# A two-block model at 256 tokens: the buffers of the main matmuls begin 64 bytes apart modulo 512 in place of on one edge

## The chip, the cores and the metric

The kernel runs on one core of one Trainium2 chip. The metric is the device time of one execution in microseconds (us); the time before is the median of three runs, 2506.98 us (2501.33 to 2507.89).

## The reference

Two residual blocks run one after the other on 256 tokens of width 2048, in float32. Cut to what matters:

```python
# block 1: attention in a sliding window, then SwiGLU
x = x + sliding_window_attention(rms_norm(x), w_qkv, ...) @ w_o
x = x + (silu(h @ w_gate) * (h @ w_up)) @ w_down          # D_FF = 5632
# block 2, layer 0: mLSTM mixer
proj = modulate(rmsnorm(x)) @ a_w_in                      # 16400 columns
x = x + gate * rmsnorm(mlstm(proj) @ a_w_out)
# block 2, layer 1: attention over bands of chunks
kv = modulate(rmsnorm(x)) @ kv_w                          # 4096 columns
x = x + gate * rmsnorm(band_attention(h @ b_w_in, kv) @ b_w_out)
```

The modulations come from a vector c times ada_w_2 and kv_ada_w_2, which the kernel sums on VectorE. Nearly all arithmetic is in the eight large products, of a 256-row activation with a weight matrix read from HBM.

## The kernel before, in words

**Precision.** Each float32 operand of a large product is split into a high part of the type float32r and a float32r remainder, and a product is three matmuls: high by high, high by low, low by high. The activations' parts stand in four lasting buffers of 16 tiles of 128 x 256: `xh` and `xl` (the normed input) and `ah` and `al` (the mixers' and the FFN's inner result). They are the lines 117 to 120.

**The weights' stream.** A weight matrix goes through in pieces of 256 rows by 512 columns (512 KB). `stream_load` (line 138) has SyncE's queue fetch a piece into one of three buffers `w`; `stream_split` (line 146) has ScalarE cast it into `wh` and VectorE subtract it into `wl`, each with four buffers that are used in turn. `do_group` (line 226) loads up to four pieces and splits up to three pieces ahead of the one in use.

**The main matmuls.** `products` (line 267) issues them, in one of two modes. In the mode "tok" the activation part is stationary (128 x 128) and 512 columns of the weight part move past it; in "wst" 128 columns of the weight part are stationary and the 256 tokens move:

```python
PE.matmul(o, h[:, c], wh[:, k], ...)      # tok
PE.matmul(o, h[:, c], wl[:, k], ...)
PE.matmul(o, l[:, c], wh[:, k], ...)
PE.matmul(o, wh[:, k, cc], h, ...)        # wst
PE.matmul(o, wh[:, k, cc], l, ...)
PE.matmul(o, wl[:, k, cc], h, ...)
```

In the profile the moving operand is named first: `mm<-wh,xh` is tok, `mm<-xh,wh` is wst. Each matmul has a weight load of its own (PEld), which runs while the matmul before it streams; what TensorE reads at one time is thus the moving operand of one matmul and the stationary one of the next. TensorE starts main matmuls in the order written, with smaller ones between them (named `bg`: transposes, attention scores, gates).

**Where the buffers stand.** The tiles are laid out in order of allocation. `xh` begins at byte 34816 of each partition, which is 68 times 512; each of `xh`, `xl`, `ah`, `al` and `big` is 16384 bytes, and each buffer of `w`, `wh` and `wl` is 4096 bytes, so all of these begin at 0 modulo 512. The slices that one matmul reads (512 bytes of a stationary part, 1024 or 2048 of a moving one) begin at 0 modulo 512 as well. Of the operands of other float32r matmuls, `onesr` begins at 128, `acch` and `accl` at 448 modulo 512, and slice kt of `wgh` and of `wgl` at 416 + 160 kt.

**Order of the work.** It is worked out when the program is built: a model of the engines' clocks (`Clock`, `Eng`) decides at which main matmul a background task advances. The model looks at the number of elements and the type, not at addresses. A second stream of pieces (`mvt`) feeds the modulation sums on VectorE (`mvacc`).

**The end.** The last product, b_w_out, writes 512 columns of two token tiles at a time; `fin_half` (line 1235) squares them on ScalarE for a sum (`sumsq`, line 458), with the squares themselves written to a junk tile `sq` that nothing reads.

Of the kernel before, what the change touches and what calls it, by code (L numbers as in the profile page):

```python
# [10 lines left out]
F32 = mybir.dt.float32  # L11
F32R = mybir.dt.float32r
# [6 lines left out]
P = 128  # L19
D = 2048  # L20
T = 256
KD = D // P
SL = 2
CW = 512
NEG = -1.0e30
EPS = 1e-6
DFF = 5632
# [53 lines left out]
def kernel(ctx: ExitStack, tc: tile.TileContext, i: dict, out: bass.AP):  # L81
# [5 lines left out]
    keep = ctx.enter_context(tc.tile_pool(name="keep", bufs=1))  # L87
    strm = ctx.enter_context(tc.tile_pool(name="strm", bufs=1))
    rest = ctx.enter_context(tc.tile_pool(name="rest", bufs=1))
    small = ctx.enter_context(tc.tile_pool(name="small", bufs=4))  # L90
    psp = ctx.enter_context(tc.tile_pool(name="psp", bufs=8, space=PSUM))

    live = [0, 0]
    mmres = [4]
    ver = {"x": [0] * KD, "a": [0] * KD}
# [18 lines left out]
    onesr = keep.tile([P, P], F32R, name="onesr")  # L114
    mods = keep.tile([P, 3, 2, KD], F32, name="mods")
    x = keep.tile([P, 2, D], F32, name="x")
    xh = keep.tile([P, KD, T], F32R, name="xh")
    xl = keep.tile([P, KD, T], F32R, name="xl")
    ah = keep.tile([P, KD, T], F32R, name="ah")
    al = keep.tile([P, KD, T], F32R, name="al")  # L120
    big = keep.tile([P, 2 * D], F32, name="big")
    raw = big.rearrange("p (k t) -> p k t", t=T)
    part = big.rearrange("p (t n) -> p t n", t=2)
# [14 lines left out]
    def stream_load(upto):  # L138
        while cnt["load"] < min(upto, len(order)):
            ch, s = order[cnt["load"]]  # L140
            w = strm.tile([P, SL, CW], F32, tag="w", bufs=3, name="w")
            ch.load(s, w)
# [3 lines left out]
    def stream_split(upto):  # L146
        while cnt["split"] < min(upto, len(order)):
            j = cnt["split"]
            w = loaded.pop(j)
            clk.cur = 0.0  # L150
            wh = strm.tile([P, SL, CW], F32R, tag="wh", bufs=4, name="wh")
            S.copy(wh, w)
            wl = strm.tile([P, SL, CW], F32R, tag="wl", bufs=4, name="wl")
            V.tensor_sub(wl, w, wh.bitcast(F32))
            split[j] = (wh, wl, clk.cur)
            cnt["split"] += 1
# [54 lines left out]
    def wload(w, r0, c0):  # L211
        def f(s, t):
            a = w[r0 + s * SL * P:r0 + (s + 1) * SL * P, c0:c0 + CW]
            nc.sync.dma_start(out=t, in_=a.rearrange("(k p) n -> p k n", p=P))
# [11 lines left out]
    def do_group(idxs):  # L226
        staged = len(idxs) > 1
        ch, s0 = order[idxs[0]]
        for k in range(s0 * SL, (s0 + len(idxs)) * SL):
            while ver[ch.need[0]][k] < ch.need[1][k]:  # L230
                stall()
        stream_load(idxs[0] + 1 + PF)
        stream_split(idxs[0] + 1 + SP)
        if s0 == 0:
            shp = [P, CW] if ch.mode == "tok" else [P, 2, T]
            while live[0] + live[1] > 6:
# [3 lines left out]
        for ts in ((0,), (1,)) if staged else ((0, 1),):  # L240
            for j, idx in enumerate(idxs):
                s = order[idx][1]
                if j and ts[0]:
                    stream_load(idx + 1 + PF)
                    stream_split(idx + SP)
                wh, wl, t_w = split.pop(idx) if ts[-1] else split[idx]
                for k in range(SL):
                    kt = s * SL + k
                    clk.cur = max(t_w, rdy[ch.need[0]][kt])
                    products(ch, kt, k, wh, wl, ts)  # L250
                    ch.k = kt + ts[-1]
                    if not staged:
                        mv_step()
                    if kt < ch.nk - 1:
                        pump()
            if s == ch.ns - 1:
                clk.cur = clk.eng["pe"]
                if ch.part is not None:
                    for t in ts:
                        ch.part(ch.ps, t)  # L260
                if ts[-1]:
                    if not (ch.done and ch.done(ch.ps)):
                        mm_free()
                    ch.ps = None
                pump()
# [52 lines left out]
    def mv_jobs():  # L318
        for lab, w, c0, b, kind, dst in (
                [("A", i["ada0"], j * CW, i["ada_b"][0:1, j * CW:(j + 1) * CW], "col", (0, j // 4, j % 4))  # L320
                 for j in range(8)]
# [134 lines left out]
        return b.rearrange("p a b -> p (a b)")  # L456

    def sumsq(junk_pool, src, dst, scale=1.0):
        j = junk_pool.tile([P, CW], F32, tag="sq", bufs=1, name="sq")
        S.activation(j, src, ACTF.Square, scale=scale, accum_out=dst)  # L460

    def xt_pair(m):
# [83 lines left out]
    ssx = rest.tile([P, 2, 4], F32, name="ssx")  # L546
# [208 lines left out]
    def resid(n, ps, pool, after):  # L755
        for t in range(2):
            c = x[:, t, n * CW:(n + 1) * CW]
            V.tensor_add(c, ps[t], c)
            sumsq(pool, c, ssx[:, t, n:n + 1])
        add_bg(after(n))  # L760
# [36 lines left out]
    pools = {}  # L797
# [50 lines left out]
    def down_part(ps, t):  # L848
        c = x[:, t, 3 * CW:]
        V.tensor_add(c, ps[t], c)  # L850
        sumsq(pools["q2"], c, ssx[:, t, 3:4])
        if t:
            add_bg(xt_raw(3, raw))
# [146 lines left out]
    def num_task(h, v):  # L1000
# [22 lines left out]
        for t in range(2):  # L1023
            sumsq(q3, nm[t], ss[:, t:t + 1], scale=rd[:, t:t + 1])
# [143 lines left out]
    def band_head(g, j):  # L1168
# [5 lines left out]
        nc.sync.dma_start(out=bi, in_=bass.AP(tensor=rel.tensor, offset=h * 383, ap=[[1, P], [1, T]]))  # L1174
        G.memset(bi[0:64, 0:64], NEG)
        yield 1
# [57 lines left out]

    def fin_half(ps, t, n):
        c = pools["yy"][:, t, n * CW:(n + 1) * CW]
        sumsq(pools["q4"], ps[t], ssx[:, t, n:n + 1])
        V.tensor_mul(c, ps[t], gt[1][:, n * CW:(n + 1) * CW])

    def fin_done(n):  # L1240
        def f(ps):
            for t in range(2):
                fin_half(ps, t, n)
        return f

    def fin_part(ps, t):
        fin_half(ps, t, 3)
        x_rstd((t,))
        for n in range(4):
            c = x[:, t, n * CW:(n + 1) * CW]  # L1250
            y = pools["yy"][:, t, n * CW:(n + 1) * CW]
            if n == 3:
                S.activation(y, y, ACTF.Copy, scale=rst[:, t:t + 1])
                G.tensor_add(c, c, y)
            else:
                V.scalar_tensor_tensor(c, y, rst[:, t:t + 1], c, op0=ALU.mult, op1=ALU.add)
        for n in range(4):
            nc.sync.dma_start(out=out[t * P:(t + 1) * P, n * CW:(n + 1) * CW], in_=x[:, t, n * CW:(n + 1) * CW])
# [39 lines left out]
    S.activation(warm, ones[:, 0:1], ACTF.Exp)  # L1298
    stream_load(1)
    stream_split(1)  # L1300
    load_x(0)
    nc.sync.dma_start(out=cols, in_=i["cols"])
# [35 lines left out]
def _lay(inputs):  # L1338
# [10 lines left out]
    r = np.arange(P)  # L1349
    lo = np.where(r[None, :] <= r[:, None], f(0), f(NEG)).astype(f)  # L1350
    up = np.where(r[None, :] > r[:, None], f(0), f(NEG)).astype(f)
    ge = np.where(r[None, :] >= r[:, None], f(0), f(NEG)).astype(f)
    inv = np.power(10000.0, -np.arange(0, 64, 2) / 64.0).astype(f)
# [33 lines left out]
```

## Time and profile before

| | |
|---|---|
| median of three runs | 2506.98 us |
| the profiled execution | 2509.79 us |
| its span, first to last instruction | 2508.0 us |
| mean granted TensorE clock in it | 0.989 |
| TensorE busy | 2438.4 us (97%) |
| VectorE busy | 1752.8 us (70%) |
| ScalarE busy | 1210.1 us (48%) |
| DMA queue of the weights | 573.42 MB, 70.8% of 16 engines |

A matmul's shown duration is longer than its share of TensorE, since matmuls are pipelined: a row "0.39" may follow the one before it by 0.23 us. What one matmul costs is therefore read from start to start. The timeline gives starts to 0.01 us, so a distance is taken over many matmuls and divided by their number. [...]

### The profile page before, as it was taken

The page shows a single profiled execution, that of the slowest core. Times are in us where ns is not written, and L with a number is a line of the kernel's source. Part 1 is how long each engine was busy: PE and PEld are TensorE (multiplying, and loading weights), DVE is VectorE, ACT ScalarE, POOL GpSimd, SP SyncE. Part 2 cuts the span into 40 slices and gives each one's busy share as a digit, 9 for nine tenths or more (in the row PEclk, how much of TensorE's full clock was granted, in tenths as well). Part 3 has the DMA queues.
Part 4 walks back from the last instruction along what each step waited for, and adds up shares of the span by engine and source line. Part 5 has one row for each costly group of instructions (what it writes and reads, how often), then busy time and mean ns, then how long its engine had stood idle before and what let it go on. Part 6 is the DMA issues. An engine that isn't in the chain of part 4 may idle for free.

```text
span 2508.0 us, 34570 instructions
## 1 busy us (share of the span) xinstructions
PE 2438.4 (97%) x12782; PEld 2076.4 (83%) x12782; DVE 1752.8 (70%) x2577; ACT 1210.1 (48%) x1654; POOL 173.4 (7%) x174
## 2 busy tenths in 40 slices
PE   8989999999999999899999999999999899999998
PEld 6867888887888888778888788888888789899986
DVE  6885777777777777768778777755454664577765
ACT  5665544334443444554445444445444544555553
POOL 0232000000000000201101100101101120000000
PEclk9989999999999999999999999999999999999999
DMA  6524788888888887568878788856556456678854
GB/s 211 157 96 143 238 285 284 286 275 279 287 283 291 285 286 267 159 213 269 264 250 273 267 286 277 261 170 192 182 169 196 151 151 186 193 254 263 259 188 153
DMA packets 319226, 575.63 MB, mean 230 GB/s; under 512 B 21680, under 2 KB 56752, under 8 KB 319056
## 3 DMA queue, kind: packets, MB, share of 16 engines
q1 hardware_dynamic: 319056, 573.42, 70.8%
q8 instruction: 100, 1.64, 0.3%
q14 instruction: 70, 0.57, 0.1%
HBM read 571.25 MB, written 2.10 MB: 229 GB/s over the span
## 4 chain that ended last, share of the span: by engine, by line
PE 77%; DVE 7%; DMA 6%; issue 4%; ACT 4%; POOL 2%; SPq 0%; ACTq 0%; DVEq 0%; POOLq 0%
PE mm L66 72%; PE bg L66 5%; DVE wl L66 3%; ACT wh L66 2%; DMA w<-in_a_w_in_dram 2%; DVE mvacc L66 2%; DMA w<-in_w_gate_dram 1%; DMA w<-in_w_down_dram 1%; POOL big L66 1%; DMA w<-in_w_qkv_dram 1%; ACT big L66 1%; POOL y L66 0%; DMA w<-in_a_w_out_dram 0%; POOL so L66 0%; ACT sq L66 0%
## 5 line engine op out<-in xcount | busy, mean ns | idle before, releaser
L66 DVE TENSOR_TENSOR wl<-w,wh 128x1024 fp32r<-128x1024 f32 x816 | 1009.3, 1244 | 620.9 <-ACT wh L66 605.4
L66 ACT CAST wh<-w 128x1024 fp32r<-128x1024 f32 x816 | 854.9, 1051 | 957.1 <-PE mm L66 598.8
L66 PE MATMUL mm<-wh,xh 128*128 128x512 f32 x1760 | 691.4, 393 | 0.0
L66 PE MATMUL mm<-wh,xl 128*128 128x512 f32 x1760 | 686.8, 390 | 3.8 <-DVE xl L66 3.8
L66 PE MATMUL mm<-wl,xh 128*128 128x512 f32 x1760 | 686.8, 390 | 3.0 <-DVE wl L66 3.0
L66 DVE SCALAR_TENSOR_TENSOR mvacc<-mvt,sc,mvacc 128x512 f32<-128x512 f32 x512 | 392.2, 766 | 10.1 <-issue 0.5
L66 PEld LDWEIGHTS mm<-wh,xl 128*128 128x128 f32 x1760 | 331.1, 188 | 74.3 <-DVE xl L66 4.7
L66 PEld LDWEIGHTS mm<-wl,xh 128*128 128x128 f32 x1760 | 331.2, 188 | 72.2 <-DVE wl L66 5.1
L66 PEld LDWEIGHTS mm<-wh,xh 128*128 128x128 f32 x1760 | 331.2, 188 | 70.5 <-issue 2.6
L66 PE MATMUL mm<-xh,wh 128*128 128x256 f32 x1280 | 370.0, 289 | 7.9 <-DVE xh L66 7.9
L66 PE MATMUL mm<-xl,wh 128*128 128x256 f32 x1280 | 367.5, 287 | 1.0 <-DVE xl L66 0.9
L66 PE MATMUL mm<-xh,wl 128*128 128x256 f32 x1280 | 365.6, 286 | 0.0
L66 PE MATMUL mm<-wh,al 128*128 128x512 f32 x864 | 337.8, 391 | 3.5 <-DVE al L66 3.5
L66 PE MATMUL mm<-wh,ah 128*128 128x512 f32 x864 | 340.3, 394 | 0.0
L66 PE MATMUL mm<-wl,ah 128*128 128x512 f32 x864 | 337.5, 391 | 0.0
L66 PEld LDWEIGHTS mm<-xh,wh 128*128 128x128 f32 x1280 | 249.2, 195 | 11.6 <-DVE xh L66 5.5
L66 PEld LDWEIGHTS mm<-xl,wh 128*128 128x128 f32 x1280 | 249.1, 195 | 4.4 <-DVE xl L66 3.5
L66 PEld LDWEIGHTS mm<-xh,wl 128*128 128x128 f32 x1280 | 249.1, 195 | 0.0
L66 PEld LDWEIGHTS mm<-wh,al 128*128 128x128 f32 x864 | 163.0, 189 | 38.1 <-DVE al L66 3.9
L66 PEld LDWEIGHTS mm<-wh,ah 128*128 128x128 f32 x864 | 162.9, 189 | 36.7 <-issue 3.3
L66 PEld LDWEIGHTS mm<-wl,ah 128*128 128x128 f32 x864 | 163.0, 189 | 33.2 <-DVE wl L66 0.3
L66 POOL TENSOR_TENSOR so<-so,sz 128x512 f32<-128x512 f32 x16 | 29.6, 1851 | 711.8 <-DVE mvacc L66 361.8
(191 smaller groups left out, 1303.2 us busy)
## 6 DMA issues: line engine op xcount, KB each, us to landing
mvt<-in_ada_dram SPq DMA_DIRECT2D x192, 512.0 KB
w<-in_a_w_in_dram SPq DMA_DIRECT2D x192, 512.0 KB
w<-in_w_gate_dram SPq DMA_DIRECT2D x88, 512.0 KB
w<-in_w_up_dram SPq DMA_DIRECT2D x88, 512.0 KB
w<-in_w_down_dram SPq DMA_DIRECT2D x88, 512.0 KB
mvt<-in_kv_ada_dram SPq DMA_DIRECT2D x64, 512.0 KB
w<-in_a_w_in_dram SPq DMA_DIRECT2D x128, 256.0 KB
w<-in_a_w_out_dram SPq DMA_DIRECT2D x64, 512.0 KB
```

Source lines behind the costliest of these rows:

```text
L66: return fn(*a, **k)
```

## The change

A helper `stepped` allocates a tile with 16 more float32 elements (64 bytes) in a row than are used and hands out the front. The four activation parts and the four buffers each of `wh` and `wl` are made with it, so that each pushes what is allocated behind it 64 bytes further: modulo 512, `xh`, `xl`, `ah`, `al` begin at 0, 64, 128, 192; `big` and the three `w` at 256; the four `wh` at 256, 320, 384, 448; the four `wl` at 0, 64, 128, 192. What is allocated later moves by 768 bytes, which is 256 modulo 512. So that it all fits, the junk tile `sq` of the last stage (2048 bytes) is given up and `fin_half` writes the squares into the first two tiles of `xh`. Numbers of instructions, shapes, loops and DMAs are as before.

```diff
+STEP = 16
...
+    def stepped(pool, k, n, **kw):
+        t = pool.tile([P, k * n + STEP], F32R, **kw)
+        return t[:, 0:k * n].rearrange("p (k n) -> p k n", n=n)
...
-    xh = keep.tile([P, KD, T], F32R, name="xh")
-    xl = keep.tile([P, KD, T], F32R, name="xl")
-    ah = keep.tile([P, KD, T], F32R, name="ah")
-    al = keep.tile([P, KD, T], F32R, name="al")
+    xh, xl, ah, al = (stepped(keep, KD, T, name=n) for n in ("xh", "xl", "ah", "al"))
...
-            wh = strm.tile([P, SL, CW], F32R, tag="wh", bufs=4, name="wh")
+            wh = stepped(strm, SL, CW, tag="wh", bufs=4, name="wh")
             S.copy(wh, w)
-            wl = strm.tile([P, SL, CW], F32R, tag="wl", bufs=4, name="wl")
+            wl = stepped(strm, SL, CW, tag="wl", bufs=4, name="wl")
...
     def sumsq(junk_pool, src, dst, scale=1.0):
-        j = junk_pool.tile([P, CW], F32, tag="sq", bufs=1, name="sq")
+        if junk_pool is None:
+            j = xh[:, 0:2].rearrange("p k t -> p (k t)")
+        else:
+            j = junk_pool.tile([P, CW], F32, tag="sq", bufs=1, name="sq")
...
-        sumsq(pools["q4"], ps[t], ssx[:, t, n:n + 1])
+        sumsq(None, ps[t], ssx[:, t, n:n + 1])
```

## Rows read from the trace of the kernel before

**Rows 1.** The page's head and its busy times by engine.

```profile
span 2508.0 us, 34570 instructions
PE 2438.4 (97%) x12782; PEld 2076.4 (83%) x12782; DVE 1752.8 (70%) x2577; ACT 1210.1 (48%) x1654; POOL 173.4 (7%) x174
```

**Rows 2.** The page's chain that ended last, by line.

```profile
PE mm L66 72%; PE bg L66 5%; DVE wl L66 3%; ACT wh L66 2%; DMA w<-in_a_w_in_dram 2%; DVE mvacc L66 2%; DMA w<-in_w_gate_dram 1%; DMA w<-in_w_down_dram 1%; POOL big L66 1%; DMA w<-in_w_qkv_dram 1%; ACT big L66 1%; POOL y L66 0%; DMA w<-in_a_w_out_dram 0%; POOL so L66 0%; ACT sq L66 0%
```

**Rows 3.** The page's groups of main matmuls: moving operand, stationary operand, shape, number, then busy us and mean ns of one.

```profile
L66 PE MATMUL mm<-wh,xh 128*128 128x512 f32 x1760 | 691.4, 393 | 0.0
L66 PE MATMUL mm<-wh,xl 128*128 128x512 f32 x1760 | 686.8, 390 | 3.8 <-DVE xl L66 3.8
L66 PE MATMUL mm<-wl,xh 128*128 128x512 f32 x1760 | 686.8, 390 | 3.0 <-DVE wl L66 3.0
...
L66 PE MATMUL mm<-xh,wh 128*128 128x256 f32 x1280 | 370.0, 289 | 7.9 <-DVE xh L66 7.9
L66 PE MATMUL mm<-xl,wh 128*128 128x256 f32 x1280 | 367.5, 287 | 1.0 <-DVE xl L66 0.9
L66 PE MATMUL mm<-xh,wl 128*128 128x256 f32 x1280 | 365.6, 286 | 0.0
L66 PE MATMUL mm<-wh,al 128*128 128x512 f32 x864 | 337.8, 391 | 3.5 <-DVE al L66 3.5
L66 PE MATMUL mm<-wh,ah 128*128 128x512 f32 x864 | 340.3, 394 | 0.0
L66 PE MATMUL mm<-wl,ah 128*128 128x512 f32 x864 | 337.5, 391 | 0.0
```

**Rows 4.** An unbroken stretch of tok matmuls in the FFN: two of TensorE's rows of the timeline (start us, duration us, ...), the first and the last of 566, and the busy times of all engines between them (PE, PEld, DVE, ACT, POOL, each with its number of instructions; then granted clock, DMA share, GB/s). The 565 of the window are those from the first row to the last but one.

```profile
732.70 0.39 PE L66 MATMUL mm<-wl,ah 128*128 128x512 f32 x1
...
860.77 0.39 PE L66 MATMUL mm<-wh,xl 128*128 128x512 f32 x1
...
733.00:860.70 127.70, 127.70 (x565) 105.75 (x564) 97.36 (x107) 50.67 (x50) 1.58 (x3) 1.00 0.86 289
```

**Rows 5.** The same for an unbroken stretch of wst matmuls in the keys of the last layer: the first and the last of 595, and the window over them.

```profile
2037.65 0.28 PE L66 MATMUL mm<-xh,wl 128*128 128x256 f32 x1
...
2108.92 0.28 PE L66 MATMUL mm<-xh,wl 128*128 128x256 f32 x1
...
2037.85:2108.95 71.10, 71.10 (x595) 71.10 (x594) 31.50 (x26) 28.77 (x31) 0.00 (x0) 1.00 0.64 192
```

**Rows 6.** wst matmuls just before, at the lower clock: the first and the last of nine in a row (eight distances), and a window over them for the granted clock.

```profile
2008.69 0.41 PE L66 MATMUL mm<-xh,wl 128*128 128x256 f32 x1
...
2010.39 0.41 PE L66 MATMUL mm<-xl,wh 128*128 128x256 f32 x1
...
2008.70:2010.38 1.68, 1.68 (x9) 1.68 (x9) 1.13 (x2) 1.51 (x3) 1.68 (x3) 0.50 0.00 0
```

**Rows 7.** The gates' matmuls (line 910): 48 in a row, float32r, 256 columns of `xh` or `xl` moving as in wst, with 40 columns of `wgh` or `wgl` stationary; the first, the last, and the main matmul after them, and the window (its 49 hold one main matmul at the front).

```profile
1060.97 0.28 PE L66 MATMUL bg<-xh,wgh 128*40 128x256 f32 x1
...
1066.46 0.28 PE L66 MATMUL bg<-xh,wgl 128*40 128x256 f32 x1
1066.58 0.40 PE L66 MATMUL mm<-wh,xh 128*128 128x512 f32 x1
...
1061.00:1066.50 5.50, 5.50 (x49) 5.38 (x48) 3.54 (x4) 0.00 (x0) 0.00 (x0) 1.00 0.67 220
```

**Rows 8.** The timeline of TensorE around one reduction of a modulation sum (`onesr` at 128 stationary, `acch` and `accl` at 448 moving) amid wst matmuls.

```profile
2400.67 0.28 PE L66 MATMUL mm<-xh,wh 128*128 128x256 f32 x1
2400.79 0.28 PE L66 MATMUL mm<-xl,wh 128*128 128x256 f32 x1
2400.91 0.28 PE L66 MATMUL mm<-xh,wl 128*128 128x256 f32 x1
2401.03 0.28 PE L66 MATMUL bg<-acch,onesr 128*128 128x256 f32 x1
2401.15 0.28 PE L66 MATMUL bg<-accl,onesr 128*128 128x256 f32 x1
2401.27 0.28 PE L66 MATMUL mm<-xh,wh 128*128 128x256 f32 x1
...
2402.22 0.28 PE L66 MATMUL mm<-xh,wl 128*128 128x256 f32 x1
```

**Rows 9.** Tok matmuls right after a group of transposes: the second one after it and the twelfth, ten matmuls later.

```profile
862.10 0.39 PE L66 MATMUL mm<-wl,xh 128*128 128x512 f32 x1
...
864.41 0.39 PE L66 MATMUL mm<-wh,xl 128*128 128x512 f32 x1
```

**Rows 10.** The page's groups of the two splits of a piece.

```profile
L66 DVE TENSOR_TENSOR wl<-w,wh 128x1024 fp32r<-128x1024 f32 x816 | 1009.3, 1244 | 620.9 <-ACT wh L66 605.4
L66 ACT CAST wh<-w 128x1024 fp32r<-128x1024 f32 x816 | 854.9, 1051 | 957.1 <-PE mm L66 598.8
```

**Rows 11.** What writes the junk tile in the last stage (duration ns shortest/median/longest, first and last start us), and a square of the same size from and to other places.

```profile
L66 ACT ACTIVATE sq<-x x32: 629/632/637, 19.9 to 2002.3; 128x512 f32<-128x512 f32 x32
...
L66 ACT ACTIVATE sq<-mm x8: 597/598/599, 2447.8 to 2497.8; 128x512 f32<-128x512 f32 x8
```

## The prediction

> **What bounds the kernel now.** I read the busy times first: TensorE is busy for 97% of the span, VectorE for 70%, ScalarE for 48% [rows 1]. The chain that ended last says the same: main matmuls hold 72% of it, 1806 us, and no other line more than 5% [rows 2]. Then the groups: 7872 main matmuls of 512 columns (tok) and 3840 of 256 (wst), 11712 in all [rows 3]. They are pipelined, so their shown durations don't add; what one costs is the distance from start to start. In the longest unbroken stretch that is 128.07 us over 565 distances, 226.7 ns, at a granted clock of 1.00, with VectorE busy 76% and the DMA engines 86% of it [rows 4]. For wst it is 71.27 us over 594, 120.0 ns [rows 5].
>
> [...]
>
> [...] The mean distance over both kinds is (7872 x 226.7 + 3840 x 120.0) / 11712 = 191.7 ns; 1806 us of chain are 9420 such distances, 80% of the main matmuls. **One nanosecond per main matmul is 9.4 us.** The profiled execution took 2509.8 us with a span of 2508.0, and stands 2.8 us above the median of the runs; sums go against the former, and 2.8 is taken off at the end.
>
> **The change, part by part.**
>
> *The junk tile.* Eight squares of 512 columns go to xh instead of a tile of their own. The eight to `sq` take 597 to 599 ns; squares of the same size from other tiles to other places take 629 to 637 [rows 11], so another address bounds it at 40 ns each, and only the last pair stands near the end: 0.1 us at most. Below, nothing suggests a gain. They wait for the last readers of xh, the main matmuls of b_w_in, which lie in front of the whole of b_w_out. I take 0.
>
> *The splits.* `w`, `wh` and `wl` now begin on different edges for the cast (1051 ns) and the subtraction (1244 ns) [rows 10]. Both engines are off the path for most of the span, yet the subtraction is 3% of the chain and the cast 2% [rows 2], together some 125 us. TensorE's queue of split pieces covers them; where that cover is gone, in those 125 us, a change of 2% in their durations, which is more than the spread of the squares in one place but less than between places, is 2.5 us either way. I take 0 and keep 2.5.
>
> *The order of the work, the DMAs, the waits.* The planner sees elements and types, which stay; nothing is moved past anything, no DMA is added, and the buffers are as many. 0.
>
> *The main matmuls.* Now moving and stationary operands begin at 0 modulo 512, always. Afterwards the distance between them differs from matmul to matmul: in tok, `wh` at 256 to 448 or `wl` at 0 to 192 stream while `xh` at 0 or `xl` at 64 is loaded (`ah` at 128, `al` at 192); in wst it is the reverse. The trace of before has no main matmul on other edges, so I bound the effect.
>
> Three rows come near. First, the gates: 48 float32r matmuls of 256 columns whose stationary slices begin on sixteen different edges. They take 5.61 us, 116.9 ns each [rows 7], a surplus of 10.2 ns in place of 13.3; but they load 40 columns and not 128. Second, a main matmul streaming from 0 while `onesr` at 128 is loaded shows 0.12 us, as its neighbours do: no effect within 0.01 us. Third, behind the pair that streams from 448, eight distances to 2402.22 take 0.95 us, 118.8 ns, although these matmuls are on the common edge again [rows 8]. [...]
>
> [...] The gates are the nearest row, since there many edges follow one another as they will in the changed kernel, so I take their 10.2 ns for both kinds: -3.1 ns x 9.4 = -29 us.
>
> [...]
>
> **The sum:** 2509.8 - 29 + 0 + 0 = 2481, less 2.8: **2478 us**. What is late next where TensorE gets 1.4% quicker: the DMA engines, 86% busy in the FFN, and VectorE, 76% [rows 4]; both have room for it.
>
> **The rivals.**
>
> *No effect.* [...] For it: the load of `onesr` at 128 changes nothing [rows 8]; 226.7 and 120.0 hold over hundreds of matmuls while ScalarE, VectorE and DMA come and go [rows 4, 5]. Against it: the gates' 116.9. Time: 2507 us, give or take 3.
>
> *Slower: the step is lost.* After a group of transposes, ten tok distances in a row take 2.31 us, 231 ns each [rows 9], though shape and edges are those of the stretch at 226.7; then the step is found again. So the even spacing on the common edge is the better state of tok, not the worse. If changing edges keep matmuls from ever falling into step, tok pays 231 - 226.7 = 4.3 ns on 80% of 7872, 27 us, and wst gains at most the 1.2 ns of 118.8 against 120.0 on 80% of 3840, 4 us: 2507 + 27 - 4 = 2530 us. The place is every tok product; the point from which it decides is a mean tok distance above 227.3 ns, where the loss of 6300 tok matmuls passes the 4 us of wst. For it: the rows at 231 are tok rows, and two thirds of all main matmuls are tok, while the gates, which speak for a gain, are of 256 columns.
>
> [...]
>
> **How the numbers follow.** A difference under 0.3% (7.5 us) can't be told from no change here. Forecast 0.34 (2478, its own range 2462 to 2495: surplus 8.5 to 12 ns); larger gain 0.13; no effect 0.24; slower 0.29. Faster by over 0.3% is 0.34 + 0.13 = 0.47, same 0.24, slower 0.29. The range that leaves out 2 in 10 runs from 2444, the half of the surplus, to 2533, the slower rival with the 2.5 us of the splits. It holds both signs because the row that says gain and the row that says loss are of different lengths of matmul, and tok, which decides, has only the latter.
>
> **What would show it.** In the timeline of the changed kernel, the distances in the FFN and in the keys of the last layer: 223.6 and 116.9 ns would be the forecast; 226.7 and 120.0 no effect; 229 to 231 in tok the lost step; 220 and 113 the larger gain. The number of instructions and the DMA bytes should be as before, and the squares of the last stage within 40 ns of 598. If the time moves while these distances don't, the reason was another: the splits' durations or the waits of the main matmuls for them would show it, and my argument would be wrong. It would be wrong in part if tok and wst moved in opposite directions.

## The result: slower by 0.9%

The changed kernel takes 2527.93 us (median of four runs, 2524.25 to 2529.52) against 2506.19 us before (four runs), a ratio of 1.0088 with a 95% interval of 1.0070 to 1.0106. The range given held it, and the direction forecast was wrong: the time is that of the second rival (2530 us), whose mechanism turned out to be the smaller part of the story.

The profile of the changed kernel: its head, busy times and chain, then the groups that answer to [rows 3] and [rows 10].

```profile
span 2522.5 us, 34570 instructions
...
PE 2460.0 (98%) x12782; PEld 2066.5 (82%) x12782; DVE 1754.8 (70%) x2577; ACT 1206.8 (48%) x1654; POOL 172.4 (7%) x174
...
PE mm L67 74%; PE bg L67 5%; DMA w<-in_a_w_in_dram 3%; DVE wl L67 3%; ACT wh L67 2%; DVE mvacc L67 1%; DMA w<-in_w_qkv_dram 1%; DMA w<-in_b_w_in_dram 1%; POOL big L67 0%; POOL so L67 0%; POOL y L67 0%; ACT big L67 0%; DVE xl L67 0%; DMA mvacc<-in_ada_b_dram 0%; ACT sq L67 0%
...
L67 DVE TENSOR_TENSOR wl<-w,wh 128x1024 fp32r<-128x1024 f32 x816 | 1009.9, 1244 | 633.3 <-ACT wh L67 625.2
L67 ACT CAST wh<-w 128x1024 fp32r<-128x1024 f32 x816 | 852.4, 1048 | 973.3 <-PE mm L67 684.2
L67 PE MATMUL mm<-wh,xh 128*128 128x512 f32 x1760 | 699.8, 398 | 0.0
...
L67 PE MATMUL mm<-xh,wh 128*128 128x256 f32 x1280 | 365.8, 286 | 8.2 <-DVE xh L67 8.2
```

The numbers of instructions are those of [rows 1]. TensorE is busy 21.6 us longer and main matmuls hold 74% of the chain, 1867 us against 1806. The splits have not moved (1244 ns both times; 1048 against 1051). The 512-column matmuls show longer rows than in [rows 3] (398 against 393 ns), the 256-column ones shorter (286 against 289): the two kinds went opposite ways.

How far, one reads from start to start. Every kernel of this study has two stretches of 575 tok matmuls in the FFN (574 distances each; the first is used here) and one of 598 wst matmuls in the keys of the last layer (597), with nothing between the matmuls. TensorE's rows of the timeline in the changed kernel, first and last of each stretch, and the windows over both (columns as in [rows 4]):

```profile
464.25 0.39 PE L67 MATMUL mm<-wl,ah 128*128 128x512 f32 x1
...
597.21 0.39 PE L67 MATMUL mm<-wh,xl 128*128 128x512 f32 x1
...
464.60:597.10 132.50, 132.50 (x574) 107.42 (x573) 99.34 (x110) 51.68 (x51) 1.58 (x3) 1.00 0.85 282
...
2050.20 0.29 PE L67 MATMUL mm<-xh,wl 128*128 128x256 f32 x1
...
2121.20 0.28 PE L67 MATMUL mm<-xh,wl 128*128 128x256 f32 x1
...
2050.20:2121.10 70.90, 70.90 (x598) 70.90 (x598) 32.07 (x27) 28.90 (x32) 0.00 (x0) 1.00 0.63 193
```

Tok: 132.96 us / 574 = **231.6 ns**, where [rows 4] give 226.7. Wst: 71.00 / 597 = **118.9 ns**, where [rows 5] give 120.0. The clock is at its full level in both (granted clock 1.00), and VectorE, ScalarE and the DMA engines are about as busy as before (VectorE 75% of the tok stretch against 76%, DMA 85% against 86%), so the loss is in how closely tok matmuls follow one another.

### The profile page after: what moved, and what is told of

It reads as the page before. It is cut to its first block, busy times and chain, and to the rows that moved or that the text cites. A ratio compares the mean times of both kernels' runs of the same rounds, so it can differ in the third digit from the quotient of the medians.

```text
span 2522.5 us, 34570 instructions
## 1 busy us (share of the span) xinstructions
PE 2460.0 (98%) x12782; PEld 2066.5 (82%) x12782; DVE 1754.8 (70%) x2577; ACT 1206.8 (48%) x1654; POOL 172.4 (7%) x174
## 4 chain that ended last, share of the span: by engine, by line
PE 79%; DVE 6%; DMA 5%; issue 4%; ACT 4%; POOL 1%; SPq 0%; ACTq 0%; DVEq 0%; POOLq 0%
PE mm L67 74%; PE bg L67 5%; DMA w<-in_a_w_in_dram 3%; DVE wl L67 3%; ACT wh L67 2%; DVE mvacc L67 1%; DMA w<-in_w_qkv_dram 1%; DMA w<-in_b_w_in_dram 1%; POOL big L67 0%; POOL so L67 0%; POOL y L67 0%; ACT big L67 0%; DVE xl L67 0%; DMA mvacc<-in_ada_b_dram 0%; ACT sq L67 0%
## 5 line engine op out<-in xcount | busy, mean ns | idle before, releaser
L67 DVE TENSOR_TENSOR wl<-w,wh 128x1024 fp32r<-128x1024 f32 x816 | 1009.9, 1244 | 633.3 <-ACT wh L67 625.2
L67 ACT CAST wh<-w 128x1024 fp32r<-128x1024 f32 x816 | 852.4, 1048 | 973.3 <-PE mm L67 684.2
L67 PE MATMUL mm<-wh,xh 128*128 128x512 f32 x1760 | 699.8, 398 | 0.0
L67 PEld LDWEIGHTS mm<-xh,wh 128*128 128x128 f32 x1280 | 243.6, 190 | 11.6 <-DVE xh L67 6.0
L67 PEld LDWEIGHTS mm<-xl,wh 128*128 128x128 f32 x1280 | 243.3, 190 | 4.7 <-DVE xl L67 3.8
L67 PEld LDWEIGHTS mm<-xh,wl 128*128 128x128 f32 x1280 | 243.2, 190 | 0.0
```

Source lines behind the costliest of these rows:

```text
L67: return fn(*a, **k)
```

## The experiments

All use the changed kernel without its stagger, in which only the junk tile is given up, and add one thing. "Difference" below is the edge from which a matmul streams minus the edge from which the next one's stationary operand is loaded, in bytes.

**The junk tile alone.**

```diff
-    xh, xl, ah, al = (stepped(keep, KD, T, name=n) for n in ("xh", "xl", "ah", "al"))
+    xh, xl, ah, al = (keep.tile([P, KD, T], F32R, name=n) for n in ("xh", "xl", "ah", "al"))
...
-            wh = stepped(strm, SL, CW, tag="wh", bufs=4, name="wh")
+            wh = strm.tile([P, SL, CW], F32R, tag="wh", bufs=4, name="wh")
```

and the same for `wl`. Expected: 

> Only the last stage's junk tile is given up; all main buffers stay on the common edge, as before. If the loss of the change comes from the main matmuls' edges (both theories below), this takes the time of before, 2506 us within 5, and 226.7 and 120.0 ns from start to start. If the squares into xh make a wait at the end, up to 22 us more.

Measured: 2507.04 us against 2505.81, ratio 1.0006 (0.9995 to 1.0017). The squares take what they took in [rows 11] (median 598 ns):

```profile
L67 ACT ACTIVATE xh<-mm x8: 597/598/599, 2447.0 to 2497.0; 128x512 fp32r<-128x512 f32 x8
```

Its tok stretch, from 461.73 to 591.86 us, is at 226.7 ns again. So the loss is in the stagger, and this kernel is a fair base for what follows.

**One half of the stagger at a time.** First `stepped` is kept for `xh`, `xl`, `ah`, `al` alone. Expected: 

> Only the four activation parts are staggered; w, wh and wl all begin at 256 modulo 512. Theory of the lost step (edges that keep changing hold the matmuls out of step): the edges now repeat every three matmuls, so a step of three can be found, the distances settle to a fixed pattern, and the time falls back to 2506 us or a little above it. Theory of the dear distance (each difference between the edge that streams and the edge that is loaded has its own price, and the common edge is a cheap one): by the means of the changed kernel for these differences, some 232 ns in tok and 118.3 in wst, 2535 us.

Then it is kept for `wh` and `wl` alone. Expected: 

> Only the buffers of wh and wl are staggered; xh, xl, ah and al all begin at 0. Lost step: the edges still change from piece to piece, so 231 ns in tok and the time of the changed kernel, 2520 to 2530 us. Dear distance: the same differences occur as in the changed kernel in other shares, 230 to 233 ns, 2515 to 2540 us. The two don't differ here; it tells which half of the change costs.

Measured: 2532.59 us for the activations alone (ratio 1.0104, 1.0089 to 1.0119) and 2521.23 us for the weights alone (1.0063, 1.0047 to 1.0080). Either half costs, and the costs don't add. The tok stretch of the first and of the second:

```profile
466.10 0.40 PE L67 MATMUL mm<-wl,ah 128*128 128x512 f32 x1
...
599.58 0.39 PE L67 MATMUL mm<-wh,xl 128*128 128x512 f32 x1
```

```profile
465.37 0.39 PE L67 MATMUL mm<-wl,ah 128*128 128x512 f32 x1
...
597.95 0.40 PE L67 MATMUL mm<-wh,xl 128*128 128x512 f32 x1
```

133.48 / 574 = 232.5 and 132.58 / 574 = 231.0 ns. The activations alone missed the expectation of the lost step: their edges repeat every three matmuls, and no cheap step was found. What the theory of the dear distance had for them (232 ns in tok, 2535 us) came out. With the weights alone there was something else, in wst: TensorE's rows where the stream goes over from a piece at an even multiple of 64 to one at an odd multiple.

```profile
2063.57 0.28 PE L67 MATMUL mm<-xh,wl 128*128 128x256 f32 x1
2063.70 0.28 PE L67 MATMUL mm<-xh,wh 128*128 128x256 f32 x1
...
2064.53 0.28 PE L67 MATMUL mm<-xl,wh 128*128 128x256 f32 x1
2064.64 0.28 PE L67 MATMUL mm<-xh,wl 128*128 128x256 f32 x1
2064.76 0.28 PE L67 MATMUL mm<-xh,wh 128*128 128x256 f32 x1
...
2065.89 0.28 PE L67 MATMUL mm<-xl,wh 128*128 128x256 f32 x1
```

From 2063.57 to 2064.53 there are eight distances, 0.96 us, 120 ns each; from 2064.76 to 2065.89 ten, 1.13 us, 113 ns. The distance changes with the piece.

**Two edges, with one difference throughout.** A tile of the difference's size is allocated between the activation parts and the stream, for 64 bytes

```diff
+    keep.tile([P, 16], F32, name="pad")
     kc = rest.tile([P, NCONST], F32, name="kc")
```

and nothing is staggered. First with 256 bytes. Expected: 

> No stagger, but two edges: xh, xl, ah, al at 0, all of w, wh and wl at 256 modulo 512. Every pair of reads has the same difference, other than zero. Lost step: nothing changes from matmul to matmul, so the step is found; the distances have a spread under 1 ns and lie at 226.7 and 120.0, 2506 us, or at another even value. Dear distance: the means of the changed kernel at this difference, 234.0 ns in tok and 118.4 in wst: 2507 + 7.3 x 6.3 - 1.6 x 3.1 = 2548 us.

Measured: 2505.63 us, ratio 0.9992 (0.9983 to 1.0002).

```profile
460.88 0.39 PE L67 MATMUL mm<-wl,ah 128*128 128x512 f32 x1
...
591.01 0.39 PE L67 MATMUL mm<-wh,xl 128*128 128x512 f32 x1
```

130.13 / 574 = 226.7 ns, the distance of [rows 4]. That looked like the lost step proven, and the dear distance, as it was priced then (234.0 ns, 2548 us), refuted: leave the edges alone and the step is there. Four other differences said otherwise.

64 bytes, expected: 

> Two edges again: activation parts at 0, all of w, wh and wl at 64 modulo 512. Theory that change from matmul to matmul is what costs: an even spacing is found as with 256, at 226.7 or 120.0 ns, 2506 us. With what the staggered weights showed beside it (within one piece, where the difference is an odd multiple of 64, wst ran evenly at 113.3 ns, with an even one at 120.0): wst at 113.3, 3840 x 6.7 x 0.8 = 20 us less; tok at 226.7 gives 2486 us, tok at 233.3 (seen there for edges 192 and 448) gives 2486 + 42 = 2528 us. Rival, the zero or the half of 512 is what is good: tok at 229 to 233, above 2515 us.

128 bytes, expected: 

> Activation parts at 0, all of w, wh and wl at 128 modulo 512. If only change from matmul to matmul costs: 226.7 and 120.0 ns, 2506 us. Rival, the zero or the half of 512 is what is good: tok at 230 to 233 ns, 2525 us or more.

192 bytes, expected: 

> Activation parts at 0, all of w, wh and wl at 192 modulo 512. If an odd multiple of 64 gives wst 113.3 whatever it is: 2486 us with tok at 226.7, 2528 with tok at 233.3. The pair of edges 192 and 448 showed tok at 233.3 evenly, so 2528 is the likelier one.

448 bytes, expected: 

> Activation parts at 0, all of w, wh and wl at 448 modulo 512, which is the mirror of 64: as 64 if only the size of the difference counts, as 192 if the direction does. wst at 113.3 in both; tok at 226.7 gives 2486 us, at 233.3 it gives 2528.

Measured: 2511.93 us for 64 (ratio 1.0018, 1.0007 to 1.0030), 2538.44 for 128 (1.0129, 1.0097 to 1.0160), 2540.63 for 192 (1.0139, 1.0115 to 1.0163), 2540.33 for 448 (1.0136, 1.0103 to 1.0169). The tok stretches with 64, with 128 and with 192:

```profile
462.84 0.39 PE L67 MATMUL mm<-wl,ah 128*128 128x512 f32 x1
...
594.23 0.40 PE L67 MATMUL mm<-wh,xl 128*128 128x512 f32 x1
```

```profile
467.73 0.39 PE L67 MATMUL mm<-wl,ah 128*128 128x512 f32 x1
...
601.65 0.39 PE L67 MATMUL mm<-wh,xl 128*128 128x512 f32 x1
```

```profile
468.80 0.39 PE L67 MATMUL mm<-wl,ah 128*128 128x512 f32 x1
...
602.73 0.41 PE L67 MATMUL mm<-wh,xl 128*128 128x512 f32 x1
```

131.39, 133.92 and 133.93 us over 574: 228.9, 233.3 and 233.3 ns. With 448 the stretch runs from 469.73 to 603.66 us, 233.3 ns too. Here nothing changes from matmul to matmul, and tok is dearer at all four differences than at 0. So a steady difference has a price in tok here, and 256 has that of 0 (226.7 ns) while 448 has that of 192 (233.3): the price seemed to depend on the difference modulo 256.

In these runs the activations stand at 0, so they don't tell the difference from the weights' own edge. The trace of the changed kernel does. There, sorted by the edges of the layout, tok matmuls followed by a load of `xh` (at 0) and of `ah` (at 128) agree at each difference, though their streaming edges are 128 bytes apart: 232.9 and 232.9 ns on average at 0, 228.4 and 229.0 at 64, 233.5 and 233.6 at 128, 232.4 and 232.5 at 192 modulo 256. Those followed by a load of `xl` and of `al` agree with each other too, within 1.1 ns, but stand up to 4 ns off the first two; what makes that gap no run shows.

The wst stretch with 64:

```profile
2045.49 0.28 PE L67 MATMUL mm<-xh,wl 128*128 128x256 f32 x1
...
2113.17 0.28 PE L67 MATMUL mm<-xh,wl 128*128 128x256 f32 x1
```

67.68 / 597 = 113.4 ns against 120.0: in wst this difference is a gain. (Tok streams the weights and loads the activations, wst the reverse, so 64 in the one is -64 in the other.) At 64 loss and gain nearly cancel in the time: 2511.93 us against 2505.89. The first theory there allowed tok 226.7 or 233.3; 228.9 is the low end of its rival's 229 to 233, with a time under that rival's 2515 us. With 192 and 448 wst took 117.8 ns in its stretch, and not the 113.3 that was expected.

**Changing edges with one difference modulo 256.** The helper's 16 elements become 64, for `wh` and `wl` alone.

```diff
-        t = pool.tile([P, k * n + STEP], F32R, **kw)
+        t = pool.tile([P, k * n + 64], F32R, **kw)
```

Expected: 

> The buffers of wh and wl begin 256 bytes further each, so their edges alternate between 0 and 256 modulo 512; the activation parts at 0. Theory of the difference modulo 256 (0 and 256 showed the same distances, 192 and 448 too): every difference is 0 modulo 256, so 226.7 and 120.0 ns though the edges change from matmul to matmul, 2506 us. Rival, change from matmul to matmul is what costs: as with the weights staggered by 64, 231 ns in tok, 2521 us.

Measured: 2506.32 us against 2507.32, ratio 0.9997 (0.9988 to 1.0007), and the tok stretch:

```profile
459.89 0.39 PE L67 MATMUL mm<-wl,ah 128*128 128x512 f32 x1
...
590.02 0.39 PE L67 MATMUL mm<-wh,xl 128*128 128x512 f32 x1
```

130.13 / 574 = 226.7 ns, though the edges alternate. The same stagger by 64 cost 0.63%. So in this run a change of edges by 256, which keeps the difference modulo 256, cost nothing.

A change by 64, which alters it, did cost something of its own, as the trace of the weights staggered by 64 shows. There the difference stays the same through a piece's twelve tok matmuls and moves by 64 to the next piece. TensorE's rows of a piece at difference 0, its first and its sixth matmul, and the first of the next piece:

```profile
483.17 0.39 PE L67 MATMUL mm<-wh,ah 128*128 128x512 f32 x1
...
484.33 0.39 PE L67 MATMUL mm<-wh,al 128*128 128x512 f32 x1
...
485.92 0.39 PE L67 MATMUL mm<-wh,ah 128*128 128x512 f32 x1
```

Five distances take 1.16 us, 232 ns each, and the next seven 1.59 us, 227 ns. Over the whole trace, the first five tok distances at difference 0 after a change or a break average 231.6 ns, and the ones after them 227.5. So in this trace the cheap spacing came back only some matmuls after such a change, as it did behind the transposes of [rows 9].

**A version that uses it.** As the last, and a piece that goes to wst matmuls stands 64 bytes further within its buffer.

```diff
+            off = STEP if order[j][0].mode == "wst" else 0
-            wh = stepped(strm, SL, CW, tag="wh", bufs=4, name="wh")
+            wh = stepped(strm, SL, CW, off, tag="wh", bufs=4, name="wh")
```

and the same for `wl`, where `stepped` returns `t[:, off:off + k * n]`. Expected: 

> As e9, and in addition a piece that goes to wst matmuls is split into the buffer's part that begins 64 bytes behind its front: tok pairs differ by 0 modulo 256, wst pairs by 64. Difference modulo 256: tok stays at 226.7 to 227, wst goes from 119.8 to the 115.1 of e5, 3840 x 4.7 x 0.8 = 14 us less than before, 2492 us. Rival, the mixed stages disturb each other (every change of mode puts tok out of step): tok at 228 or more, no gain, 2506 us or slower.

Measured: 2496.55 us against 2507.32, ratio **0.9955 (0.9941 to 0.9970)**: faster than both kernels, by somewhat less than expected (2492 us). Its tok and wst stretches:

```profile
461.31 0.39 PE L67 MATMUL mm<-wl,ah 128*128 128x512 f32 x1
...
591.44 0.39 PE L67 MATMUL mm<-wh,xl 128*128 128x512 f32 x1
...
2030.28 0.28 PE L67 MATMUL mm<-xh,wl 128*128 128x256 f32 x1
...
2100.60 0.28 PE L67 MATMUL mm<-xh,wl 128*128 128x256 f32 x1
```

Tok stays at 130.13 / 574 = 226.7 ns. Wst is at 70.32 / 597 = 117.8 ns in this stretch, where the kernel with one edge at 64 had 113.4 at the same difference. Over the whole trace wst averages 116.2 ns against 119.8 before; 3.6 ns on 80% of 3840 are 11 us, and 10.8 were measured. So at one difference wst had more than one spacing; what chooses between them was not tried.

**Half of 64.** Two runs with the stream at 32 and at 480. Expected: 

> Activation parts at 0, all of w, wh and wl at 32 modulo 512. If an edge acts by the 64 bytes it lies in: as 0, 226.7 and 120.0 ns, 2506 us. If it acts by its distance in bytes: between 0 and 64, tok 227 to 229 and wst 115 to 120, 2500 to 2512 us, or something lower in both.

And: 

> Activation parts at 0, all of w, wh and wl at 480 modulo 512, the mirror of 32. If an edge acts by the 64 bytes it lies in: as 448, tok 233.3 and wst 117.7, 2540 us. If by its distance in bytes: between 448 and 0, tok 227 to 233, 2506 to 2540 us.

Measured: 2541.7 us (ratio 1.0138, 1.0120 to 1.0156) and 2538.97 us (1.0127, 1.0106 to 1.0149). The tok stretch with 32:

```profile
469.48 0.39 PE L67 MATMUL mm<-wl,ah 128*128 128x512 f32 x1
...
603.41 0.39 PE L67 MATMUL mm<-wh,xl 128*128 128x512 f32 x1
```

133.93 / 574 = 233.3 ns. Both guesses for 32 missed: it neither acts as 0 nor lies between 0 and 64. With 480 the first guess, that it acts as 448, came out in tok (469.99 to 603.92 us, 233.3 ns) and in the time; wst took 116.7 ns in its stretch in place of 117.7.

## Why the prediction was right or wrong

**What bounds the kernel, and what the edit can act on: right.** Main matmuls bind (74% of the chain), their distance from start to start does move with the edges (tok from 226.7 to 231.6 ns, wst from 120.0 to 118.9), and nothing else moved: instructions, splits and junk tile came out at nothing, as costed (junk tile alone 1.0006).

**The step that failed: "so I take their 10.2 ns for both kinds."** That takes 3.1 ns off both kinds, the gates' 116.9 [rows 7] against 120.0; tok rose by 4.9 ns and wst fell by 1.1. No run shows what the columns of a matmul take alone, and so none shows the 10.2 ns, the 13.3, or the half of 13.3 at which the range begins, as a surplus over that. By an estimate from [rows 4] and [rows 5], where 256 columns more make 226.7 - 120.0 = 106.7 ns, either kind had 13.3 ns over its columns before, and tok has 231.6 - 213.4 = 18.2 and wst 118.9 - 106.7 = 12.2 after. The gates' row was one of 256 streaming columns with 40 columns to load; it had the sign of wst and nothing of tok, where two thirds of the main matmuls are. The prediction named that weakness in its last line on the range, and still priced tok by it. What each difference costs tok, the runs with one difference show: 226.7, 228.9, 233.3 and 233.3 ns at 0, 64, 128 and 192 modulo 256. Before, all pairs had the cheapest of the four. In the changed kernel the four weight buffers run through all four differences in equal shares, and the mean of the four is 230.6.

The other 1.0 ns up to 231.6 comes from the pairs with difference 0. Sorted by the edges of the layout, the four kinds of tok distance in the changed kernel average 231.7, 229.4, 232.5 and 233.0 ns in its whole trace: three cost what they cost alone, within 1 ns, while the pairs at 0 do not get their 226.7 among neighbours at other differences. Two more traces show the same: the pairs at 0 average 232.0 ns with the activations alone staggered and 229.4 with the weights alone, where the last seven distances of the piece shown above took 227 ns. In the changed kernel a difference stays for one or two matmuls only.

**The second rival: the number right, its mechanism a smaller part.** It gave 231 ns in tok, a small gain in wst and 2530 us; measured are 231.6, 118.9 and 2527.9. Its price came from matmuls that were out of step on the common edge [rows 9], and its reason was that changing edges keep them so. Edges that change by 256 cost nothing (0.9997), and edges that don't change, at 128 or 192, cost more than the change did (1.0129, 1.0139). So most of the loss, 3.9 of 4.9 ns, is that tok is dearer at 64, 128 and 192 even where the difference stays; the lost step is the 1.0 ns of the pairs at 0. That [rows 9], the price of lost steps alone, and the mean over the differences agree within 1 ns was luck.

**A row that could not speak.** The prediction counted the load of `onesr` at 128 for no effect, since its row shows 0.12 us as its neighbours do [rows 8]. Rows are given to 0.01 us, which is 10 ns; every effect measured here is between 1 and 7 ns, so one row can show none of them.

**The conversion to time: right in kind.** 4.9 ns on 7872 tok matmuls less 1.1 ns on 3840 are 38.6 - 4.2 = 34.4 us of TensorE; the 80% on the chain make 27.5 us, and 21.7 were measured (17.5 to 26.6 by the interval). Part of the gap is that the stretches overstate the mean: over the whole traces at full clock tok went from 227.0 to 231.6 and wst from 119.8 to 118.9, which makes 26 us. Another part may be the clock. Its mean was 0.990 to 0.993 in the four runs after, 0.991 on average, and 0.987 to 0.991 in the 17 runs of the kernel before that stand beside the last experiments, 0.989 on average; by an estimate from these means, 0.002 or 0.003 of 2520 us, that is 5 to 8 us in favour of the changed kernel. Why it was higher, and so whether this belongs to the change, no run shows. Waits for pieces are no smaller in the chain: w_gate and w_down, 1% each in [rows 2], are gone from it, but a_w_in went from 2 to 3% and b_w_in came in with 1%.

## What to carry to other kernels

Before laying out buffers by a stagger, measure the distance from start to start at each single difference between what streams and what is loaded. Here spreading over four differences brought 231.6 ns in tok, where the mean of the four alone is 230.6 and the common edge had the lowest of them, 226.7. A row taken from one shape of matmul was no price for another here: the gates' 256 columns said 3.1 ns less, and the 512 columns of tok took 4.9 more; look for the row in the shape that holds most of the chain, even if it is a disturbed one. And where the two modes of a kernel want different edges, as tok (226.7 ns at 0, 228.9 at 64) and wst (120.0 and 113.4) do here, give each its own; that took 0.45% off.

## What was not expected of the hardware

In tok, where a kernel keeps one difference, the distance went with that difference modulo 256 bytes (226.7 ns at 0 and at 256; 233.3 at 192 and at 448; a stagger of the weights by 256 at 0.9997, by 64 at 1.0063; no other pair was tried), and 32 bytes are already enough to take tok from 226.7 to 233.3 ns. In wst the difference alone doesn't settle it: 113.4 and 117.8 ns were measured at the same one.

Four of the spacings are, within 0.1 ns, whole multiples of 6.67 ns, a unit estimated from these spacings themselves: 226.7 is 34 of them, 233.3 is 35, 120.0 is 18, and the 113.4 of wst is 17 (113.3). The 228.9 of tok and the 117.8 of wst are not, but three distances, one round of the three products, are: 686.7 ns is 103 units and 353.4 is 53. So against before, tok at 128 or 192 takes one such unit more, and wst at its best one less. Whether the chip has such a unit, and why tok and wst want different edges, no run shows.
